# Hybrid encoder, first mixer: projecting each attention group in two parts, with three attention blocks between them

## Chip, cores and metric

The kernel runs on one core of one Trainium2 chip. The metric is the device time of one execution in microseconds (us). Engines: PE (TensorE), DVE (VectorE), ACT (ScalarE), POOL (GpSimd), and SP, whose queue issues most of the DMAs.

## What is computed

Two encoder layers over 1024 tokens of width 1024. Each has a token mixer and a gated feed-forward network. The change touches the first mixer alone: windowed attention with 16 query heads of 64 in four groups that share one key/value head each, rotary position, one sink per head, and beside it four cross-attention heads of 128 into 256 memory tokens.

```
q, k, v, xq = split(u @ w_in, [1024, 1280, 1536])
q, k = rope(q), rope(k)                    # v: no rotary
# block n of 128 queries sees keys of blocks n-1, n, n+1, |i - j| <= 128
s = q @ k.T * d ** -0.5 ;  m = max(max(s), sink)
p = exp(s - m) / (sum(exp(s - m)) + exp(sink - m))
o = p @ v
y = concat([o, memory_cross_attn(xq, mem_kv)]) @ w_out
```

## The kernel before

Every product of fp32 precision is built from high and low parts: `split` (lines 85 to 87) copies a tile to its high part on ACT and subtracts it on DVE for the low part, and `mm3` (lines 80 to 83) issues three matmuls. The normalised input stands transposed in `uh` and `ul`.

The tokens are eight tiles of 128. For each group of heads `proj(g)` (line 252) loads four weight units (`wunit`, line 69, in a ring of four slots), and for each tile `t` multiplies 24 times into a PSUM bank `pj` of 384 columns (lines 81 to 83, two such banks), applies the rotary products on DVE (lines 274 and 275), adds them on POOL into `rq` (lines 276 and 277), and splits the values (lines 279 and 280). After four tiles it turns them: PE transposes `rq` into the one bank `ptq` (line 286), first the two pairs of query heads and then the keys, and ACT and DVE split them into `qs` (lines 294 to 297) and into `kh`, `kl`. Keys and values of even and odd groups lie in different pools, so two groups can be alive at once.

`attend(g)` (line 300) goes through eight blocks `n` of 128 queries. A block takes, for each of four heads, two score matmuls into one of two `ps` banks (lines 315 and 316) and a masked maximum on DVE (line 318); then exponentials on ACT (line 325), scaling on ACT and DVE (lines 331 and 333), transposes into `pt` (line 338), `split` into `ph`, `pl`, two value products into the one bank `po` (lines 341 and 342) and an output sum (lines 344 and 345). Inner blocks have 384 keys, the first and last 256. Two blocks at a time go to `oT` in DRAM.

A cross unit (`cross_unit`, line 185) is one cross head and half of the tokens: 24 matmuls of 512 columns into a `pj` bank, a split into `xh`, `xl` (one buffer), scores into `ps`, a maximum (line 204), exponentials, transposes and products with the memory's values. There are eight; `XU` says how many stand behind each half of a group's attention.

The program's text is projection and attention in turn, group after group. A scheduler turns it into one fixed order for each engine: it takes what is ready, earlier text first, so that products of the next group fill attention's waits. The release of the pools that hold `pj` and `ptq` after the last projection gives their banks to the output projection `WOut` (line 371), whose `open` runs products into banks `pb` beside the last attention. Weights for the output projection take the same ring.

Of the kernel before, what the change touches and what calls it, by code (L numbers as in the profile page):

```python
# [6 lines left out]
F32 = mybir.dt.float32  # L7
# [9 lines left out]
P = 128  # L17
T = 1024
# [12 lines left out]
MEM_POOL = 1  # L31
QKV_POOL = (0, 2, 2, 2)

XU = [(0, 2), (0, 2), (2, 2), (0, 0)]
HX = [(0,) * 6, (0,) * 6] + [(0, 0, 1, 1, 0, 0), (0,) * 6] * 2 + [(0, 0, 1, 1, 0, 0), (0, 1, 1, 0, 0, 0)]


# [9 lines left out]
def build(tc, A, out):  # L47
# [37 lines left out]
    def split(h, l, src):  # L85
        act.copy(h, src)  # L86
        dve.tensor_tensor(l, src, h.bitcast(F32), op=ALU.subtract)  # L87
# [139 lines left out]
    def window():  # L227
# [21 lines left out]

        units = [(h, b) for h in range(4) for b in range(2)]  # L250

        def proj(g):
            us = [wunit(A["wqkv"][g, u], 768, eng=pool if u < QKV_POOL[g] else None) for u in range(4)]
            qs = [[None] * 2 for _ in range(4)]
            kvp = ap_ if g % 2 else ea
            kh = kvp.tile([P, T], F32R, tag="kh", bufs=1, name="kh")
            kl = kvp.tile([P, T], F32R, tag="kl", bufs=1, name="kl")
            v = kvp.tile([P, NT, P], F32R, tag="v", bufs=1, name="v")
            for b in range(2):
                rqs = []  # L260
                for tt in range(4):
                    t = 4 * b + tt
                    ps = psq.tile([P, 384], F32, tag="pj", bufs=2, name="pj")
                    for k in range(KT):
                        wh, wl = us[k // 2]
                        c = slice((k % 2) * 384, (k % 2 + 1) * 384)
                        m = slice(t * P, (t + 1) * P)
                        mm3(ps, uh[:, k, m], ul[:, k, m], wh[:, c], wl[:, c], k == 0, k == KT - 1)
                    t1 = ea.tile([P, 320], F32, tag="t1", bufs=1, name="t1")
                    t2 = ea.tile([P, 320], F32, tag="t2", bufs=1, name="t2")  # L270
                    rq = ea.tile([P, 384], F32, tag="rq", bufs=5, name="rq")
                    cb = bc(cos[:, t, :].unsqueeze(1).unsqueeze(1), [P, 5, 2, 32])
                    sb = bc(sin[:, t, :, :].unsqueeze(1), [P, 5, 2, 32])
                    dve.tensor_tensor(c4(t1), c4(ps[:, :320]), cb, op=ALU.mult)
                    dve.tensor_tensor(c4(t2), c4(ps[:, :320])[:, :, ::-1, :], sb, op=ALU.mult)
                    pool.tensor_tensor(rq[:, :320], t1, t2, op=ALU.add)
                    done = pool.tensor_tensor(rq[:, 320:], t1[:, 256:], t2[:, 256:], op=ALU.add)
                    sum_steps[0].send(done)
                    act.copy(v[:, t, :64], ps[:, 320:])
                    dve.tensor_tensor(v[:, t, 64:], ps[:, 320:], v[:, t, :64].bitcast(F32), op=ALU.subtract)  # L280
                    rqs.append(rq)
                hs = slice(b * 512, (b + 1) * 512)
                for w in range(3):
                    tp = psq.tile([P, 4, P], F32, tag="ptq", bufs=1, name="ptq")
                    for tt in range(4):
                        pe.transpose(tp[:, tt, :], rqs[tt][:, w * P:(w + 1) * P], ident)
                    tp = tp.rearrange("p a b -> p (a b)")
                    if w == 2:
                        split(kh[:, hs], kl[:, hs], tp)
                    else:  # L290
                        lo, hi = slice(0, 64), slice(64, 128)
                        q0, q1 = [ap_.tile([P, 512], F32R, tag="qs", bufs=8, name="qs") for _ in range(2)]
                        qs[2 * w][b], qs[2 * w + 1][b] = q0, q1
                        act.copy(q0[lo], tp[lo])
                        dve.tensor_tensor(q0[hi], tp[lo], q0[lo].bitcast(F32), op=ALU.subtract)
                        act.copy(q1[hi], tp[hi])
                        dve.tensor_tensor(q1[lo], tp[hi], q1[hi].bitcast(F32), op=ALU.subtract)
            return qs, kh, kl, v

        def attend(g, qkv):  # L300
            qs, kh, kl, v = qkv
            for b in range(2):
                for nn in range(4):
                    if nn % 2 == 0:
                        o = ap_.tile([64, 4, 256], F32, tag="o", bufs=2, name="o")
                    n = 4 * b + nn
                    lo, hi = max(n - 1, 0), min(n + 2, NT)
                    w = (hi - lo) * P
                    mo = (lo - (n - 1)) * P
                    sm = ap_.tile([P, 4, 384], F32, tag="sm", bufs=3, name="sm")  # L310
                    st = {x: ap_.tile([P, 4], F32, tag=x, name=x) for x in ("mx", "nm", "es", "su", "rd")}
                    for j in range(4):
                        s = psp.tile([P, 384], F32, tag="ps", bufs=2, name="ps")
                        m = slice(nn * P, (nn + 1) * P)
                        pe.matmul(s[:, :w], qs[j][b][:, m], kh[:, lo * P:hi * P], start=True, stop=False)
                        pe.matmul(s[:, :w], qs[j][b][:, m], kl[:, lo * P:hi * P], start=False, stop=True)
                        hd = 4 * g + j
                        dve.tensor_tensor_reduce(out=sm[:, j, :w], in0=s[:, :w], in1=wmask[:, mo:mo + w],
                                                 scale=1.0, scalar=sk8[:, hd:hd + 1], op0=ALU.add, op1=ALU.max,
                                                 accum_out=st["mx"][:, j:j + 1])  # L320
                    dve.tensor_scalar_mul(st["nm"], st["mx"], -0.125)
                    dve.tensor_tensor(st["es"], sk[:, 4 * g:4 * g + 4], st["nm"], op=ALU.add)
                    act.activation(st["es"], st["es"], AF.Exp)
                    for j in range(4):
                        act.activation(sm[:, j, :w], sm[:, j, :w], AF.Exp, bias=st["nm"][:, j:j + 1], scale=0.125,
                                       accum_out=st["su"][:, j:j + 1])
                    dve.tensor_tensor(st["su"], st["su"], st["es"], op=ALU.add)
                    dve.reciprocal(st["rd"], st["su"])
                    for j in range(4):
                        if j < 2:  # L330
                            act.activation(sm[:, j, :w], sm[:, j, :w], AF.Copy, scale=st["rd"][:, j:j + 1])
                        else:
                            dve.tensor_scalar_mul(sm[:, j, :w], sm[:, j, :w], st["rd"][:, j:j + 1])
                    po = psp.tile([P, 4, P], F32, tag="po", bufs=1, name="po")
                    for c in range(hi - lo):
                        tp = psp.tile([P, 4, P], F32, tag="pt", bufs=2, name="pt")
                        for j in range(4):
                            pe.transpose(tp[:, j, :], sm[:, j, c * P:(c + 1) * P], ident)
                        ph, pl = pair("p", c)
                        split(ph, pl, tp.rearrange("p a b -> p (a b)"))  # L340
                        pe.matmul(po, v[:, lo + c, :], ph, start=c == 0, stop=False)
                        pe.matmul(po, v[:, lo + c, :], pl, start=False, stop=c == hi - lo - 1)
                    ov = o[:, :, (nn % 2) * P:(nn % 2 + 1) * P]
                    act.copy(ov, po[64:])
                    dve.tensor_tensor(ov, po[:64], ov, op=ALU.add)
                    if nn % 2 == 1:
                        ts_ = slice((n - 1) * P, (n + 1) * P)
                        for hp in range(2):
                            nc.sync.dma_start(
                                oT[0][2 * g:2 * g + 2, hp * 64:(hp + 1) * 64, ts_].rearrange("a d t -> d a t"),  # L350
                                o[:, hp::2, :])
                for _ in range(XU[g][b]):
                    xh_, xb_ = units.pop(0)
                    if xb_ == 0:
                        xhead[0] = cross_head(0, xh_, ea, ea.tile([P, 2, 256], F32, tag="kv", bufs=1, name="kv"))
                    cross_unit(0, xh_, xb_, xhead[0], ap_, tags, ea, pair)

        cur = proj(0)
        dve.tensor_scalar_mul(sk8, sk, 8.0)
        for g in range(3):  # L360
            attend(g, cur)
            cur = proj(g + 1)
        psq.release()
        ea.release()
        attend(3, cur)
        wo0.open(3, 2)
        psp.release()
        ap_.release()
# [1004 lines left out]
```

## Time and profile before

| | |
|---|---|
| median of 3 runs | 2715.87 us (2713.88 to 2719.8) |
| profiled execution | 2715.91 us |
| its span | 2714.1 us |
| mean granted PE clock | 0.992 |
| busy: PE, DVE, ACT, POOL | 97%, 67%, 51%, 17% |
| first mixer, about | 67 to 497 us of the span |

Lines of the profile name the line of the kernel, the engine, the operation, the output and inputs by the program's names, and shapes. Matmuls overlap: PE counts as busy while any matmul is in flight, so that a busy PE need not be issuing at its densest rate. The granted clock is 1.00 at full speed. Idle time in front of an instruction stands in square brackets with what ended it.

### The profile page before, as it was taken

To read this page: it belongs to the slowest core of one execution; us is meant where nothing else is said; L and a number is where in the kernel's file an instruction comes from. 1 tells how busy PE (TensorE), PEld (TensorE's weight loads), DVE (VectorE), ACT (ScalarE), POOL (GpSimd) and SP (SyncE) were. 2 spreads that over 40 slices of the span, in tenths; PEclk is the share of its full clock that TensorE was granted. 3 is DMA by queue.
4 is the path that set the end of the run, shared out by engine and by line. 5 is a ranking of instruction groups with operands and counts; after the bars stand their busy time and mean duration, and the time that the engine had idled before them with its cause. 6 is when DMAs were issued, how large, how long until landed. Compare 5 with 4: busy or idle time off the path is not lost. (4 is left out here: it accounts for less than half of the span.)

```text
span 2714.1 us, 39502 instructions
## 1 busy us (share of the span) xinstructions
PE 2638.7 (97%) x14496; PEld 2204.5 (81%) x14496; DVE 1828.5 (67%) x3042; ACT 1391.6 (51%) x2556; POOL 468.4 (17%) x520
## 2 busy tenths in 40 slices
PE   8999999999999999999999999999899999999998
PEld 7888887788888888887877888878688788888887
DVE  6588787678565565487695768769567756566447
ACT  6367667545444444454454545545454544444443
POOL 1231110211111100031132222212121111110013
PEclk9999999999999999999999999999999999999999
DMA  7683213667777757673243432111476777775666
GB/s 284 209 179 84 60 52 100 188 190 181 210 197 196 205 149 255 195 256 124 69 150 106 111 88 67 52 51 34 125 219 174 188 209 206 202 201 155 226 194 233
DMA packets 215316, 432.25 MB, mean 159 GB/s; under 512 B 20561, under 2 KB 77265, under 8 KB 209489
## 3 DMA queue, kind: packets, MB, share of 16 engines
q1 hardware_dynamic: 188128, 335.07, 38.3%
q0 software_dynamic: 24544, 90.19, 15.9%
q10 hardware_dynamic: 2448, 4.46, 0.4%
q8 instruction: 114, 1.87, 0.3%
q14 instruction: 82, 0.66, 0.1%
HBM read 335.79 MB, written 117.96 MB: 167 GB/s over the span
## 5 line engine op out<-in xcount | busy, mean ns | idle before, releaser
L87 DVE TENSOR_TENSOR wl<-st,wh 128x1024 fp32r<-128x1024 f32 (+1 forms) x238 | 262.6, 1110 | 326.7 <-ACT wh L86 321.6
L86 ACT CAST wh<-st 128x1024 fp32r<-128x1024 f32 (+1 forms) x238 | 222.5, 937 | 295.9 <-PE X L535 195.9
L81 PE MATMUL pj<-uh,wh 128*128 128x512 f32 x512 | 205.2, 401 | 6.3 <-DVE xl L87 2.5
L535 PE MATMUL X<-wl,wh 128*128 128x512 f32 x528 | 204.8, 390 | 0.3 <-DVE wl L87 0.3
L535 PE MATMUL X<-wh,wl 128*128 128x512 f32 x528 | 204.6, 389 | 0.0
L82 PE MATMUL pj<-ul,wh 128*128 128x512 f32 x512 | 202.7, 396 | 0.1
L83 PE MATMUL pj<-uh,wl 128*128 128x512 f32 x512 | 202.2, 395 | 0.0
L535 PE MATMUL X<-wh 128*128 128x512 f32 x528 | 198.8, 390 | 1.4 <-ACT c L908 1.1
L81 PE MATMUL pj<-wh,uh 128*128 128x384 f32 (+1 forms) x512 | 190.4, 373 | 0.4 <-DVE v L280 0.4
L82 PE MATMUL pj<-wl,uh 128*128 128x384 f32 (+1 forms) x512 | 186.4, 364 | 0.0
L83 PE MATMUL pj<-wh,ul 128*128 128x384 f32 (+1 forms) x512 | 186.3, 365 | 0.0
L77 DVE TENSOR_TENSOR wl<-st,wh 128x1024 fp32r<-128x1024 f32 (+1 forms) x92 | 119.0, 1301 | 23.3 <-ACT wh L76 22.8
L535 PE MATMUL V<-uh,wh 128*128 128x512 f32 x344 | 133.8, 389 | 0.0
L535 PE MATMUL V<-ul,wh 128*128 128x512 f32 x344 | 133.8, 389 | 0.0
L535 PE MATMUL V<-uh,wl 128*128 128x512 f32 x344 | 133.8, 389 | 0.0
L76 ACT CAST wh<-st 128x1024 fp32r<-128x1024 f32 (+1 forms) x99 | 100.1, 1016 | 50.8 <-PE pj L82 31.0
L81 PEld LDWEIGHTS pj<-uh,wh 128*128 128x128 f32 x512 | 97.4, 190 | 26.7 <-DVE xl L87 2.9
L535 PEld LDWEIGHTS X<-wh 128*128 128x128 f32 x528 | 99.1, 188 | 22.8 <-ACT c L908 1.5
L535 PEld LDWEIGHTS X<-wl,wh 128*128 128x128 f32 x528 | 99.1, 188 | 21.0 <-DVE wl L87 0.7
L535 PEld LDWEIGHTS X<-wh,wl 128*128 128x128 f32 x528 | 99.1, 188 | 20.7
L1134 POOL TENSOR_TENSOR E<-EP,q 128x256 f32<-128x256 f32 x64 | 49.2, 769 | 372.3 <-DVE EP L1127 280.3
L83 PEld LDWEIGHTS pj<-uh,wl 128*128 128x128 f32 x512 | 97.0, 189 | 19.6
(347 smaller groups left out, 7274.4 us busy)
## 6 DMA issues: line engine op xcount, KB each, us to landing
st<-hid SPq DMA_DIRECT2D x154, 256.0 KB, 3.1
st<-in_ffw_dram SPq DMA_DIRECT2D x108, 256.0 KB, 3.1
w2s<-in_ffw_dram POOLq DMA_DIRECT2D x24, 1024.0 KB, 7.9
st<-in_ffw_dram SPq DMA_DIRECT2D x46, 512.0 KB, 4.1
hid<-tt SPq DMA_DIRECT2D x88, 256.0 KB, 4.6
st<-w2s SPq DMA_DIRECT2D x88, 256.0 KB, 3.3
sx<-in_ffw_dram SPq DMA_DIRECT2D x84, 256.0 KB, 3.9
sy<-in_ffw_dram SPq DMA_DIRECT2D x42, 512.0 KB, 6.3
```

The source lines that it names most:

```text
L76: act.copy(h[:, :n], raw)
L77: (eng or dve).tensor_tensor(l[:, :n], raw, h[:, :n].bitcast(F32), op=ALU.subtract)
L81: pe.matmul(o, ah, bh, start=first, stop=False)
L82: pe.matmul(o, ah, bl, start=False, stop=False)
L83: pe.matmul(o, al, bh, start=False, stop=last)
L86: act.copy(h, src)
L87: dve.tensor_tensor(l, src, h.bitcast(F32), op=ALU.subtract)
L535: pe.matmul(o, x, y, start=new, stop=e, skip_group_check=not first)
L1134: pool.tensor_tensor(gl, pl_, ql, op=ALU.mult)
```

## The change

The function `proj` becomes a class with two methods: `project(t)` computes one tile, and `turn(b)` transposes and splits one half, now keys first and then the two pairs of query heads. `attend` takes a list of blocks. The order of the text in each group is: five tiles, the turn of the first half, attention blocks 0 to 2, three tiles, the turn of the second half, and for groups 0 to 2 attention blocks 3 to 7 and cross units. The cross units stand behind the whole of a group's attention, 2, 2 and 4 of them; before it was 2 behind the second half of groups 0 and 1, and 2 behind each half of group 2. In group 3, blocks 3 to 7 follow the release of the two pools, as all eight blocks did before. The arithmetic of a tile, a block and a unit is unchanged. The core of the diff:

```diff
-XU = [(0, 2), (0, 2), (2, 2), (0, 0)]
+XU = (2, 2, 4)
...
-                for w in range(3):
+                for w in (2, 0, 1):
...
-                for _ in range(XU[g][b]):
+        def cross(n):
+            for _ in range(n):
...
-        cur = proj(0)
-        dve.tensor_scalar_mul(sk8, sk, 8.0)
-        for g in range(3):
-            attend(g, cur)
-            cur = proj(g + 1)
+        cur = Group(0)
+        for g in range(4):
+            for t in range(5):
+                cur.project(t)
+            if g == 0:
+                dve.tensor_scalar_mul(sk8, sk, 8.0)
+            cur.turn(0)
+            attend(cur, range(0, 3))
+            for t in range(5, 8):
+                cur.project(t)
+            cur.turn(1)
+            if g < 3:
+                attend(cur, range(3, 8))
+                cross(XU[g])
+                cur = Group(g + 1)
         psq.release()
         ea.release()
-        attend(3, cur)
+        attend(cur, range(3, 8))
         wo0.open(3, 2)
```

More of the change, by code (lines that the diff above doesn't have):

```diff
@@ L250, in window @@
         units = [(h, b) for h in range(4) for b in range(2)]
[L252 to L281, printed above, removed]
@@ new lines, in window, with __init__, project, turn @@
+        class Group:
+            def __init__(self, g):
+                self.g = g
+                self.us = [wunit(A["wqkv"][g, u], 768, eng=pool if u < QKV_POOL[g] else None) for u in range(4)]
+                self.qs = [[None] * 2 for _ in range(4)]
+                kvp = ap_ if g % 2 else ea
+                self.kh = kvp.tile([P, T], F32R, tag="kh", bufs=1, name="kh")
+                self.kl = kvp.tile([P, T], F32R, tag="kl", bufs=1, name="kl")
+                self.v = kvp.tile([P, NT, P], F32R, tag="v", bufs=1, name="v")
+                self.rqs = {}
+            def project(self, t):
+                v = self.v
+                ps = psq.tile([P, 384], F32, tag="pj", bufs=2, name="pj")
+                for k in range(KT):
+                    wh, wl = self.us[k // 2]
+                    c = slice((k % 2) * 384, (k % 2 + 1) * 384)
+                    m = slice(t * P, (t + 1) * P)
+                    mm3(ps, uh[:, k, m], ul[:, k, m], wh[:, c], wl[:, c], k == 0, k == KT - 1)
+                t1 = ea.tile([P, 320], F32, tag="t1", bufs=1, name="t1")
+                t2 = ea.tile([P, 320], F32, tag="t2", bufs=1, name="t2")
+                rq = ea.tile([P, 384], F32, tag="rq", bufs=5, name="rq")
+                cb = bc(cos[:, t, :].unsqueeze(1).unsqueeze(1), [P, 5, 2, 32])
+                sb = bc(sin[:, t, :, :].unsqueeze(1), [P, 5, 2, 32])
+                dve.tensor_tensor(c4(t1), c4(ps[:, :320]), cb, op=ALU.mult)
+                dve.tensor_tensor(c4(t2), c4(ps[:, :320])[:, :, ::-1, :], sb, op=ALU.mult)
+                pool.tensor_tensor(rq[:, :320], t1, t2, op=ALU.add)
+                done = pool.tensor_tensor(rq[:, 320:], t1[:, 256:], t2[:, 256:], op=ALU.add)
+                sum_steps[0].send(done)
+                act.copy(v[:, t, :64], ps[:, 320:])
+                dve.tensor_tensor(v[:, t, 64:], ps[:, 320:], v[:, t, :64].bitcast(F32), op=ALU.subtract)
+                self.rqs[t] = rq
+            def turn(self, b):
@@ L282, in proj @@
                 hs = slice(b * 512, (b + 1) * 512)
-                for w in range(3):
+                for w in (2, 0, 1):
                     tp = psq.tile([P, 4, P], F32, tag="ptq", bufs=1, name="ptq")
                     for tt in range(4):
-                        pe.transpose(tp[:, tt, :], rqs[tt][:, w * P:(w + 1) * P], ident)
+                        pe.transpose(tp[:, tt, :], self.rqs[4 * b + tt][:, w * P:(w + 1) * P], ident)
                     tp = tp.rearrange("p a b -> p (a b)")
@@ L288, in proj @@
                     if w == 2:
-                        split(kh[:, hs], kl[:, hs], tp)
+                        split(self.kh[:, hs], self.kl[:, hs], tp)
                     else:
@@ L292, in proj @@
                         q0, q1 = [ap_.tile([P, 512], F32R, tag="qs", bufs=8, name="qs") for _ in range(2)]
-                        qs[2 * w][b], qs[2 * w + 1][b] = q0, q1
+                        self.qs[2 * w][b], self.qs[2 * w + 1][b] = q0, q1
                         act.copy(q0[lo], tp[lo])
@@ L297, in proj @@
                         dve.tensor_tensor(q1[lo], tp[hi], q1[hi].bitcast(F32), op=ALU.subtract)
[L298 to L311, printed above, removed]
-                    for j in range(4):
[L313 to L351, printed above, removed]
-                for _ in range(XU[g][b]):
[L353 to L356, printed above, removed]
@@ L358, in window, with attend @@
-        cur = proj(0)
-        dve.tensor_scalar_mul(sk8, sk, 8.0)
-        for g in range(3):
-            attend(g, cur)
-            cur = proj(g + 1)
+        def attend(x, blocks):
+            g, qs, kh, kl, v = x.g, x.qs, x.kh, x.kl, x.v
+            for n in blocks:
+                b, nn = divmod(n, 4)
+                if nn % 2 == 0:
+                    x.o = ap_.tile([64, 4, 256], F32, tag="o", bufs=2, name="o")
+                o = x.o
+                lo, hi = max(n - 1, 0), min(n + 2, NT)
+                w = (hi - lo) * P
+                mo = (lo - (n - 1)) * P
+                sm = ap_.tile([P, 4, 384], F32, tag="sm", bufs=3, name="sm")
+                st = {x: ap_.tile([P, 4], F32, tag=x, name=x) for x in ("mx", "nm", "es", "su", "rd")}
+                for j in range(4):
+                    s = psp.tile([P, 384], F32, tag="ps", bufs=2, name="ps")
+                    m = slice(nn * P, (nn + 1) * P)
+                    pe.matmul(s[:, :w], qs[j][b][:, m], kh[:, lo * P:hi * P], start=True, stop=False)
+                    pe.matmul(s[:, :w], qs[j][b][:, m], kl[:, lo * P:hi * P], start=False, stop=True)
+                    hd = 4 * g + j
+                    dve.tensor_tensor_reduce(out=sm[:, j, :w], in0=s[:, :w], in1=wmask[:, mo:mo + w],
+                                             scale=1.0, scalar=sk8[:, hd:hd + 1], op0=ALU.add, op1=ALU.max,
+                                             accum_out=st["mx"][:, j:j + 1])
+                dve.tensor_scalar_mul(st["nm"], st["mx"], -0.125)
+                dve.tensor_tensor(st["es"], sk[:, 4 * g:4 * g + 4], st["nm"], op=ALU.add)
+                act.activation(st["es"], st["es"], AF.Exp)
+                for j in range(4):
+                    act.activation(sm[:, j, :w], sm[:, j, :w], AF.Exp, bias=st["nm"][:, j:j + 1], scale=0.125,
+                                   accum_out=st["su"][:, j:j + 1])
+                dve.tensor_tensor(st["su"], st["su"], st["es"], op=ALU.add)
+                dve.reciprocal(st["rd"], st["su"])
+                for j in range(4):
+                    if j < 2:
+                        act.activation(sm[:, j, :w], sm[:, j, :w], AF.Copy, scale=st["rd"][:, j:j + 1])
+                    else:
+                        dve.tensor_scalar_mul(sm[:, j, :w], sm[:, j, :w], st["rd"][:, j:j + 1])
+                po = psp.tile([P, 4, P], F32, tag="po", bufs=1, name="po")
+                for c in range(hi - lo):
+                    tp = psp.tile([P, 4, P], F32, tag="pt", bufs=2, name="pt")
+                    for j in range(4):
+                        pe.transpose(tp[:, j, :], sm[:, j, c * P:(c + 1) * P], ident)
+                    ph, pl = pair("p", c)
+                    split(ph, pl, tp.rearrange("p a b -> p (a b)"))
+                    pe.matmul(po, v[:, lo + c, :], ph, start=c == 0, stop=False)
+                    pe.matmul(po, v[:, lo + c, :], pl, start=False, stop=c == hi - lo - 1)
+                ov = o[:, :, (nn % 2) * P:(nn % 2 + 1) * P]
+                act.copy(ov, po[64:])
+                dve.tensor_tensor(ov, po[:64], ov, op=ALU.add)
+                if nn % 2 == 1:
+                    ts_ = slice((n - 1) * P, (n + 1) * P)
+                    for hp in range(2):
+                        nc.sync.dma_start(
+                            oT[0][2 * g:2 * g + 2, hp * 64:(hp + 1) * 64, ts_].rearrange("a d t -> d a t"),
+                            o[:, hp::2, :])
@@ new lines, in cross @@
+        def cross(n):
+            for _ in range(n):
+                xh_, xb_ = units.pop(0)
+                if xb_ == 0:
+                    xhead[0] = cross_head(0, xh_, ea, ea.tile([P, 2, 256], F32, tag="kv", bufs=1, name="kv"))
+                cross_unit(0, xh_, xb_, xhead[0], ap_, tags, ea, pair)
+        cur = Group(0)
[13 more added lines that the diff above has]
+                cur = Group(g + 1)
```

## The prediction

> **What bounds the kernel now.** I read the page first, then the busy time by stretches of the first mixer, then TensorE's (PE's) timeline inside them, then VectorE's (DVE's) groups. From the page, the span and PE's line:
>
> ```profile
> span 2714.1 us, 39502 instructions
> PE 2638.7 (97%) x14496; PEld 2204.5 (81%) x14496; DVE 1828.5 (67%) x3042; ACT 1391.6 (51%) x2556; POOL 468.4 (17%) x520
> ```
>
> PE is the bound, but "busy" is a union of overlapping matmuls, so I price PE by the distance between starts in dense stretches. From PE's timeline (start, duration, instruction):
>
> ```profile
> 313.01 0.39 PE L82 MATMUL pj<-ul,wh 128*128 128x512 f32 x1
> 313.24 0.39 PE L83 MATMUL pj<-uh,wl 128*128 128x512 f32 x1
> 322.46 0.28 PE L83 MATMUL ps<-kvh,xl 128*128 128x256 f32 x1
> 322.58 0.28 PE L81 MATMUL ps<-kvh,xh 128*128 128x256 f32 x1
> 395.37 0.60 PE L217 MATMUL pt<-ident,xp 128*128 128x128 f32 x4
> 395.80 0.60 PE L286 MATMUL ptq<-ident,rq 128*128 128x128 f32 x4
> 398.00 0.33 PE L82 MATMUL pj<-wl,uh 128*128 128x384 f32 x1
> 398.17 0.33 PE L83 MATMUL pj<-wh,ul 128*128 128x384 f32 x1
> ```
>
> A matmul costs 0.23 us at 512 columns, 0.17 at 384, 0.12 at 256, and a transpose 0.11 (0.43 for four). I call the sum of instructions at these prices dense work. Next the stretches of the mixer (start:end, length, busy time of each engine, granted clock, DMA):
>
> ```profile
> 70.00:80.00 10.00, 7.44 (x42) 6.96 (x41) 3.59 (x8) 0.98 (x3) 2.83 (x4) 1.00 0.50 146
> 100.00:115.00 15.00, 10.99 (x50) 9.49 (x49) 11.11 (x26) 7.39 (x18) 9.54 (x12) 0.77 0.52 169
> 115.00:313.47 198.47, 194.23 (x1112) 172.50 (x1111) 154.51 (x426) 135.10 (x349) 38.95 (x52) 1.00 0.53 132
> 313.47:326.05 12.58, 9.92 (x55) 7.29 (x53) 11.63 (x40) 10.79 (x32) 0.00 (x0) 1.00 0.01 2
> 326.05:402.18 76.13, 75.36 (x448) 69.67 (x449) 58.01 (x155) 50.75 (x133) 9.93 (x14) 0.98 0.12 32
> 402.18:428.68 26.50, 18.65 (x73) 12.45 (x71) 22.67 (x64) 20.79 (x51) 1.14 (x2) 0.81 0.42 136
> 428.68:480.00 51.32, 51.32 (x258) 43.35 (x259) 34.38 (x93) 32.52 (x81) 0.00 (x0) 1.00 0.34 97
> ```
>
> Counting PE's records in these rows at the dense prices gives 6.8, 7.7, 184.8, 8.2, 71.9, 11.1 and 50.0 us. The losses are therefore 3.2, 7.3, 13.7, 4.3, 4.2, 15.4 and 1.3 us. Two rows show one state: at 313 and at 402 PE has only attention to do, and DVE is busy 92% and 86% of the time. Everywhere else PE is nearly full and DVE waits. So the mixer's time is its dense work plus what is lost where attention has no projection or output product to run beside it. A change of order can win or lose only there.
>
> DVE's instructions in the mixer, by form (line, operation, output and input, count, busy us, mean ns of one, idle before); these means are the prices below:
>
> ```profile
> L87 DVE TENSOR_TENSOR pl<-pt,ph 128x512 fp32r<-128x512 f32 x104 | 70.6, 683 | 22.4 <-ACT ph L86 22.1
> L318 DVE CUSTOM_DVE_ANT_0 sm<-ps,wmask,sk 128x384 f32<-128x384 f32 x96 | 57.2, 610 | 16.4 <-PE ps L316 14.2 <-PE pt L338 1.7
> L345 DVE TENSOR_TENSOR o<-po,o 64x512 f32<-64x512 f32 x32 | 21.7, 679 | 7.9 <-ACT o L344 7.8
> L333 DVE TENSOR_SCALAR sm<-sm,rd 128x384 f32<-128x384 f32 x48 | 18.5, 427 | 0.4
> L318 DVE CUSTOM_DVE_ANT_0 sm<-ps,wmask,sk 128x256 f32<-128x256 f32 x32 | 14.5, 475 | 2.1 <-PE ps L316 2.1
> L297 DVE TENSOR_TENSOR qs<-ptq,qs 64x512 fp32r<-64x512 f32 x16 | 11.1, 693 | 4.7 <-ACT qs L296 4.4
> L204 DVE TENSOR_REDUCE nm<-ps 128x2 f32<-128x512 f32 x16 | 10.7, 682 | 0.5 <-PE ps L83 0.4
> L318 DVE DVE_READ_ACCUMULATOR2_ANT mx<- 128x1 f32 x128 | 10.3, 80 | 0.0
> L322 DVE TENSOR_TENSOR es<-sk,nm 128x4 f32<-128x4 f32 x32 | 5.6, 174 | 0.3
> L274 DVE TENSOR_TENSOR t<-pj,cos 128x320 f32<-128x320 f32 x32 | 15.5, 484 | 12.9 <-PE pj L83 12.7
> L87 DVE TENSOR_TENSOR ol<-or,oh 128x768 fp32r<-128x768 f32 x6 | 5.7, 958 | 4.1 <-ACT oh L86 4.1
> L77 DVE TENSOR_TENSOR xwl<-st,xwh 128x1024 fp32r<-128x1024 f32 x2 | 2.4, 1216 | 0.0
> L87 DVE TENSOR_TENSOR ol<-or,oh 128x256 fp32r<-128x256 f32 x5 | 2.1, 426 | 0.9 <-ACT oh L86 0.8
> ```
>
> **What the change moves.** Arithmetic, instruction counts and DMAs stay. The scheduler writes out an order for each engine. Between the two programs these orders differ, outside the mixer, in the first products of the following FFN only, by exchanges inside a stretch where PE is full, which I price at nothing. The cross heads' loads on SP's queue move with their units, but their weights are still split ahead of group 2's first scores, and the DMA share in the row from 313 is 0.01, so I price that at nothing too. Four places in the mixer remain.
>
> *First projection.* Before, the first transpose of `rq` stands right behind the second tile's products and waits for GpSimd. In the new order a whole third tile (24 matmuls, 4.1 us) stands between.
>
> ```profile
> 77.79 0.33 PE L286 MATMUL ptq<-ident,rq 128*128 128x128 f32 x1 [2.11 <-POOL rq L276]
> 78.56 0.41 PE L81 MATMUL pj<-wh,uh 128*128 128x384 f32 x1 [0.45 <-DVE v L280]
> ```
>
> Both waits go: -2.6 us; 4.1 us of cover against 2.1 needed, and nothing else is late.
>
> *First attention blocks.* Before, the blocks wait for the last key split; these are two of the waits that make the row from 100:
>
> ```profile
> 106.19 0.50 PE L315 MATMUL ps<-kh,qs 128*128 128x256 f32 x2 [1.14 <-ACT kh L86]
> 109.02 0.45 PE L286 MATMUL ptq<-ident,rq 128*128 128x128 f32 x1 [2.33 <-DVE kl L87]
> ```
>
> In the new order keys are turned first and the first score product stands inside the last tile, so these two waits go. But the fifth score product needs one of two `ps` banks back, and DVE's queue has a query split, a weight split and two rotary products ahead of the reduction that frees it: 0.69 + 1.2 + 1.0 + 0.6, about 3.5 us. Bounds: 0 to -7.3 (the whole loss of the row); I take -2.3, the loss less this wait and 1.5 us of slow clock (the value is nearer to the waits of the row that stay in kind than to nothing lost).
>
> *Group 2.* This is the largest term. A cross unit's query product stays in a `pj` bank until the `x` operands of the unit before are used, and there are two such banks. With three units' products issued, two wait in both banks, and no projection tile of group 3, nor the fourth unit, can start until the second unit's operands are split. That split waits for the first unit's scores. Before, units 5 and 6 (of 8) stand behind block 3 of group 2, so only 12.58 us pass:
>
> ```profile
> 326.05 0.50 PE L81 MATMUL pj<-uh,wh 128*128 128x512 f32 x1 [2.49 <-DVE xl L87]
> 314.63 0.61 DVE L318 CUSTOM_DVE_ANT_0 sm<-ps,wmask,sk 128x384 f32<-128x384 f32 x1
> 325.31 0.69 DVE L87 TENSOR_TENSOR xl<-pj,xh 128x512 fp32r<-128x512 f32 x1 [0.24 <-ACT xh L86]
> ```
>
> With all four units behind block 7, the scores of the first of them stand behind blocks 3 to 7. The new PE order between the last product of the third unit and the first of the fourth has 34 score products at 384 and 8 at 256, 63 transposes, 33 value products, 4 turns and 12 cross scores: 5.8 + 1.0 + 6.9 + 7.5 + 0.4 + 1.4 = 23.1 us dense. DVE's share, by the groups above: 17 wide and 4 narrow reductions with their reads 10.4 + 1.9 + 1.7; 14 splits 9.6; 11 scalings 4.6; 5 output sums 3.4; two query splits, one `x` split and two cross maxima 3.4; 26 small ones 4.4: 39.4 us. What that takes is read from the same stretch of before, where the same count gives 13.4 us from the reduction at 314.63 on: the split ends at 326.00, 11.4 us later (0.85 of the sum, since instructions overlap), and 12.6 us pass from PE's last product (0.94). For 39.4 that is 33.5 and 37.0; I take 35.3. The loss is 35.3 - 23.1 = 12.2 against 4.3 now: +7.9. Ends: 33.5 gives +6.1, the full 39.4 gives +12.0. Nothing gives it back: after it PE has projection and cross work for 60 us, but before that work ran with 4.2 us lost in 76, so there was little to save.
>
> *The end.* In group 3 the halves come too late to help. The scheduler puts the first score products of block 0 into the last two tiles only, so seven blocks still follow the last projection, with the output projection's products (`pb`) as the only cover. Before, these begin in earnest at 428.68. In the new order they begin behind the scores of block 5, where DVE has 38.6 us of instructions since the last tile, against 28.3 before. That is: 19 reductions with reads (12.9), 7 splits (4.8), 10 scalings (4.1), 2 output sums, 4 query and 1 key splits (4.7), 3 weight splits (3.6), 5 operand splits of the output projection (two at 768 columns, two at 512, one at 256: 3.7), 20 small (3.4), one tile's rotary (1.4). Before, 28.3 took 26.5 (0.94): now 36.2. Dense PE work in it is 17.1 (11.1 before), so the loss is 19.1 against 15.4: +3.7. At 0.85 it is 32.8 and +0.3; at the full sum +6.1.
>
> Sum: -2.6 - 2.3 + 7.9 + 3.7 = +6.7. The profiled execution took 2715.91 us (span 2714.1 and 1.8 around it), equal to the median of 2715.87; so 2722.6, say **2723**. By the faster pace alone it would be -2.6 - 2.3 + 6.1 + 0.3 = +1.5.
>
> [...] In the row from 313 the granted clock is 1.00 with PE busy 79%; in the rows from 100 and 402 it is 0.77 and 0.81, though the longest single wait in the first is 2.33 us. [...]
>
> **Rivals.**
> *The clock falls through group 2's stretch.* If PE ran it at half speed, its 23.1 us would be 46.2, more than DVE's 35.3: 2722.6 + 10.9 = 2733.5. For it: 0.81 in the row from 402, where PE is busy 70%. Against: 1.00 in the same stretch of before.
>
> *Faster.* Every half now keeps three tiles in reserve while attention runs. If that ended the scattered losses (13.7 us in 115 to 313 and 4.2 in 326 to 402), the time would be 2722.6 - 17.9 = 2704.7. It decides once 12.2 of these 17.9 us go. Against: DVE has the same work there (154.51 of 198.47 us), and before, eight tiles of the next group are in reserve already.
>
> *No change.* At the faster pace, and with the opening's waits gone wholly (-7.3 for -2.3): -2.6 - 7.3 + 6.1 + 0.3 = -3.5, or 2712.4; with the -2.3 it is 2717.4.
>
> *The change does not do what it says.* Partly so, and counted above: in groups 1 and 2 the scheduler mixed next tiles into attention before, and in group 3 the blocks come too late.
>
> **How the numbers follow.** About 0.2% (5.4 us) is what a measurement of this kernel can tell from no change: 2710.5 to 2721.3. Forecast 0.55, clock 0.08, no change 0.24, faster 0.13. The forecast's own ends are -2.6 - 7.3 + 6.1 + 0.3 = -3.5 and -2.6 + 0 + 12.0 + 6.1 = +15.5, so 2712 to 2731; its middle lies above 2721.3, and a small part of it is moved to "same" against the clock's share. The range takes in the clock's 2733.5 and stops short of the faster case: 2711 to 2735. Slower 0.62, same 0.25, faster 0.13.
>
> **What would show it.** Right: the waits at 77.79 and 109.02 are gone; in group 2 one stretch of 33 to 40 us without a `pj` matmul in which DVE is over 85% busy, ended by a wait of PE for `xl`; the next 60 us nearly dense; behind the last tile more than 26.5 us to dense `pb` work. Wrong: that stretch under 25 us, the clock under 0.9 in it, or PE's loss from 115 to group 2's block 2 far from 13.7.

## The result, and the profile after

The changed kernel takes 2731.27 us (median of 5 runs, 2727.25 to 2733.16) against 2715.87 (5 runs, 2711.23 to 2719.8) before: a ratio of 1.0055, 95% interval 1.0041 to 1.0069. It is slower, by 15.4 us where 6.7 were forecast. The kernel before also ran beside every experiment below; over those later runs its median lies at 2718.1 to 2718.9. The changed kernel did not run beside those; against them the difference would be 13 us.

The first lines of the page after:

```profile
span 2729.5 us, 39511 instructions
PE 2645.6 (97%) x14496; PEld 2210.9 (81%) x14496; DVE 1827.6 (67%) x3042; ACT 1392.7 (51%) x2556; POOL 466.0 (17%) x520
```

The work is the same: equal counts of matmuls and of DVE instructions, DVE as busy as before. What grew is time in which PE issues nothing. The stretches of the mixer after, cut at the same events as in the prediction (start:end, length, busy time of each engine, granted clock, DMA):

```profile
100.00:115.00 15.00, 11.56 (x58) 10.44 (x57) 9.90 (x24) 7.66 (x17) 9.30 (x12) 0.83 0.45 138
115.00:315.24 200.24, 194.52 (x1118) 174.32 (x1117) 158.09 (x437) 137.11 (x356) 38.77 (x52) 1.00 0.53 132
315.24:353.88 38.64, 31.10 (x157) 22.00 (x155) 32.40 (x104) 33.01 (x90) 0.00 (x0) 0.96 0.08 21
353.88:415.68 61.80, 59.51 (x354) 55.66 (x354) 36.82 (x86) 28.43 (x71) 9.02 (x14) 1.00 0.11 35
415.68:444.50 28.82, 19.44 (x76) 14.51 (x76) 26.78 (x72) 22.80 (x60) 2.12 (x2) 0.76 0.46 149
444.50:510.00 65.50, 62.71 (x313) 51.92 (x313) 39.65 (x98) 41.14 (x95) 0.00 (x0) 1.00 0.30 80
```

The third row is the one to read: 38.6 us in which PE has only attention, where the same place took 12.58 us before. PE's timeline at its two ends, and DVE's at the second:

```profile
315.01 0.39 PE L83 MATMUL pj<-uh,wl 128*128 128x512 f32 x1
...
353.88 0.50 PE L81 MATMUL pj<-uh,wh 128*128 128x512 f32 x1
...
353.14 0.68 DVE L87 TENSOR_TENSOR xl<-pj,xh 128x512 fp32r<-128x512 f32 x1
```

No `pj` product starts between 315.01 and 353.88, and the one at 353.88 starts 0.06 us after the split of the unit before it ends (353.14 + 0.68). The fourth row shows why the time is not given back. PE is full there, but DVE is busy 36.82 of 61.80 us, 60%, where in the corresponding stretch before (the row from 326.05) it was busy 58.01 of 76.13. Attention had been worked off in the third row, so the projections that were held back now ran with little attention beside them.

What PE lost by stage, in us: length less its matmuls at the dense prices, counted anew in all four kernels in the same way (for before this gives 12.9 for the stretch that the prediction put at 13.7). The two kernels on the right are the first two experiments below.

| stage | before | changed | halves only | units only |
|---|---|---|---|---|
| 60 to 115 | 9.9 | 9.6 | 9.0 | 10.7 |
| 115 to group 2's stretch | 12.9 | 13.8 | 14.1 | 14.4 |
| that stretch | 4.2 | 15.0 | 3.1 | 16.6 |
| from there to the last tile | 4.2 | 3.6 | 3.7 | 8.9 |
| last tile to dense `pb` work | 15.5 | 17.3 | 19.4 | 17.9 |
| to the end of the mixer's losses | 5.9 | 4.2 | 2.2 | 5.0 |
| sum | 52.6 | 63.5 | 51.5 | 73.5 |

The first product of the next stage (`X`, in the feed-forward network) moves from 594.36 to 606.01 us, by 11.65. The other 3.7 us of the profiled difference lie behind it: 2.8 of them at one place in the network, where a wait of PE is 1.2 us longer (2.23 for 1.06) and a lower clock follows (1.00 at the same place before):

```profile
1062.00:1079.00 17.00, 14.77 (x59) 11.84 (x58) 7.41 (x12) 8.48 (x16) 0.00 (x0) 0.90 0.57 191
```

### The profile page after: what moved, and what is told of

Its sections match the earlier page's. It is cut to its first block, busy times and chain, and to the rows that moved or that the text cites. A ratio compares the mean times of both kernels' runs of the same rounds, so it can differ in the third digit from the quotient of the medians.

```text
span 2729.5 us, 39511 instructions
## 1 busy us (share of the span) xinstructions
PE 2645.6 (97%) x14496; PEld 2210.9 (81%) x14496; DVE 1827.6 (67%) x3042; ACT 1392.7 (51%) x2556; POOL 466.0 (17%) x520
```

## The experiments

Theory 1: the four cross units behind block 7 of group 2 cost the time, because units whose products are issued hold both `pj` banks until the one buffer of `x` operands is free. Theory 2: the halves cost it. Theory 3: the loss lies outside the mixer. After the first four runs theory 1 was split: 1a, a freed bank gives its gain to the time; 1b, what PE gains by running ahead of attention is owed where the projections end.

### The two parts of the change, each alone

Halves only:

```diff
-XU = (2, 2, 4)
+XU = ((0, 2), (0, 2), (2, 2))
...
-                attend(cur, range(3, 8))
-                cross(XU[g])
+                attend(cur, range(3, 4))
+                cross(XU[g][0])
+                attend(cur, range(4, 8))
+                cross(XU[g][1])
```

> The changed kernel with the cross units of group 2 put back to two behind block 3 and two behind block 7; the halves stay in all four groups. Theory 1 (the four units behind block 7 are the cost: PE lost 15.5 us in the 38.6 us without a projection product, against about 5 in the kernel before): that stretch shrinks to 12 to 15 us and the time falls by about 10, to 2721 (2718 to 2724). Theory 2 (the halves cost it: keys turned first, three tiles held back): it stays at 2728 or above. Theory 3 (the loss is outside the mixer, a clock drop in the first FFN): it stays within 3 us of the changed kernel's 2731.

Units only, on the kernel before:

```diff
-XU = [(0, 2), (0, 2), (2, 2), (0, 0)]
+XU = [(0, 2), (0, 2), (0, 4), (0, 0)]
```

> The kernel before, whole groups, with only the cross units of group 2 all behind block 7. Theory 1: in the new order 48 score products, 28 value products, 54 transposes and 12 cross scores stand between the third and the fourth unit, 21.6 us dense; a stretch of 34 to 38 us without a projection product, 12 to 16 us lost there against 4.3, time 2725 to 2728. Theory 2 (halves): 2714 to 2718, no change. Theory 3: no change in the mixer, 2716.

Measured: halves only 2717.21 us, just under theory 1's range, ratio to before 0.9995 (0.9986 to 1.0004); units only 2736.49, ratio 1.0071 (1.0059 to 1.0084). Group 2's stretch in halves only, then in units only:

```profile
315.77:326.75 10.98, 9.05 (x53) 6.66 (x51) 9.37 (x28) 9.46 (x25) 0.00 (x0) 1.00 0.08 24
```

```profile
315.83:354.88 39.05, 30.39 (x149) 22.06 (x147) 32.95 (x111) 32.66 (x91) 0.00 (x0) 0.91 0.07 14
354.88:423.10 68.22, 64.58 (x360) 59.09 (x361) 36.45 (x80) 29.54 (x74) 8.10 (x12) 0.95 0.10 32
```

The stretch comes and goes with the units' place, and the time with it. Theories 2 and 3 fall: the halves alone cost nothing. Whether they save something beside the four units is not shown, since the ratios of the changed kernel (1.0041 to 1.0069) and of units only overlap. Units only costs 18 us, 6 more than the upper end that was expected: its stretch takes 39 us where 34 to 38 were expected, and in the 68 us behind it 8.9 are lost where the changed kernel loses 3.6, again with DVE little busy (36.45 of 68.22).

### The same four units in group 1

```diff
-XU = (2, 2, 4)
+XU = (2, 4, 2)
```

> The changed kernel with the four units behind block 7 of group 1 and two behind that of group 2. Theory 1 (four units in a row hold both pj banks through blocks 3 to 7, wherever they stand): one stretch of 36 to 40 us without a projection product in group 1 and none over 15 us in group 2; about 10 us lost against halves_only, 2727 (2724 to 2731). Rival: only late in the mixer is it not given back, since here two more groups of projections follow in which attention can catch up: 2716 to 2720.

Measured: 2724.74 us, ratio 1.0019 (1.0010 to 1.0029).

```profile
225.68:262.12 36.44, 28.93 (x147) 21.68 (x146) 29.91 (x97) 31.62 (x88) 0.00 (x0) 0.91 0.07 15
262.12:315.00 52.88, 50.57 (x301) 46.89 (x300) 31.79 (x77) 23.76 (x65) 7.32 (x12) 1.00 0.33 73
```

The stretch is there, in group 1, with 14.5 us lost, and no stretch of over 8 us in group 2. The time lies in theory 1's range, at its lower end, and above the rival's. Counted as in the table, the mixer loses 59.5 us, 6.9 more than before, though the stretch alone lost 14.5: with more groups to come some of the loss is given back, not all.

### Taking away what holds the banks

Three buffers for the `x` operands. The room for them came from the load of the memory's keys and values, first by sharing the units' output buffer, then by a buffer of the weights' stage:

```diff
-            pl, n = (ea, 1) if kind == "x" else (ap_, 2)
+            pl, n = (ea, 3) if kind == "x" else (ap_, 2)
...
-... ea.tile([P, 2, 256], F32, tag="kv", bufs=1, name="kv"))
+... ea.tile([P, 512], F32, tag="xo", bufs=1, name="kv").rearrange("p (a b) -> p a b", a=2))        # x_three
+... stg.tile([P, 1024], F32, tag="st", name="kv")[:, :512].rearrange("p (a b) -> p a b", a=2))    # x_three_stage
```

> The changed kernel with three buffers in place of one for the x operands of the cross units (to make room, the memory's keys and values are loaded into the buffer of the units' output, so a head's load waits for the output of the unit before). This takes away what holds the pj banks. Theory 1: no stretch of over 15 us without a projection product in group 2; the last units' scores then fall behind the last tile, where PE has 24.8 us dense beside about 34 of DVE, a loss of 9 against 17.7 in the changed kernel: 2731 - 14 - 8 = 2709, at most 2719 if the tail gains nothing. If the units' place alone matters and not the bank: stays at 2726 or above.

> The changed kernel with three buffers for the x operands, as in x_three, but the memory's keys and values now go through a buffer of the weights' stage and not through the units' output. x_three had no stretch in group 2 but two new waits of 5.7 and 6.2 us behind a head's load. Theory 1a (what PE loses is set by the bank alone): those waits go too, 2717 to 2719 at most, less if the tail wins. Theory 1b (attention that PE runs ahead of is owed, and is paid where the projections end): the waits go (-12), but behind the last tile PE has 23 us dense beside about 48 us of DVE, 45 at 0.94, so 22 us are lost there as against 17.7 in the changed kernel: 2721 (2718 to 2726).

Measured: the first 2733.73 us, ratio 1.0060 (1.0047 to 1.0072); the second 2713.61, ratio 0.9985 (0.9975 to 0.9995). Neither has such a stretch in group 2: no gap between projection products there is longer than 8 us. The first still missed theory 1's time and lies where the units' place alone was to put it. The second, with the units in the same place, rules that reading out; what the first has in addition is a load that waits for the output of the unit before. PE's and ACT's timelines there:

```profile
415.05 0.80 PE L81 MATMUL ps<-kvh,xh 128*128 128x256 f32 x2 [6.19 <-ACT kvh L86]
...
408.90 0.58 ACT L223 COPY xo<-po 128x512 f32<-128x512 f32 x1 [1.67 <-PE po L83]
...
414.38 0.62 ACT L86 CAST kvh<-kv 128x512 fp32r<-128x512 f32 x1 [4.90 <-DMA kv<-kvd]
```

The output is copied at 408.9, stored, and only then the next head's load may start; ACT and PE stand for 5 to 6 us. With the load through the stage these waits are gone, and so is the whole loss of the change. The stretches of the second kernel:

```profile
115.00:260.00 145.00, 144.81 (x856) 135.04 (x855) 114.20 (x308) 93.94 (x246) 35.17 (x47) 1.00 0.62 153
315.00:381.10 66.10, 65.33 (x394) 59.36 (x393) 57.72 (x167) 53.66 (x143) 7.03 (x12) 1.00 0.15 36
381.10:425.00 43.90, 34.52 (x158) 24.83 (x156) 38.61 (x107) 32.50 (x86) 2.19 (x2) 0.88 0.40 124
425.00:505.00 80.00, 76.25 (x366) 62.18 (x365) 47.05 (x110) 49.71 (x115) 4.78 (x4) 0.98 0.39 110
```

PE is busy in all of 115 to 260, and the last tile ends at 381 instead of 402 (before) or 416 (changed). But 43.9 us pass from there to dense `pb` work, against 26.5 before. Of the 17.4 us more, 4.8 are lost (20.3 for 15.5) and the rest is PE work that stood ahead of the last tile before. The loss there is near the 22 that 1b gave. The time is all the same below 1b's range, and what 1a gave as its upper end holds.

### What is owed at the end

Halves only with two `x` buffers, and the kernel before with its last two units moved behind group 3's last tile:

```diff
-XU = [(0, 2), (0, 2), (2, 2), (0, 0)]
+XU = [(0, 2), (0, 2), (2, 0), (0, 0)]
...
         for g in range(3):
             attend(g, cur)
             cur = proj(g + 1)
+        cross(2)
         psq.release()
```

> The halves with the units of group 2 in their old places (halves_only), and two x buffers, keys and values through the stage. In x_three the second buffer took the scattered losses of groups 0 and 1 from 11 us (130 to 260 us) to 2. Theory 1a: that gain is kept, 2717 - 9 = 2708. Theory 1b: attention then lags by as much, the last stretch grows by about 9, and the time stays at 2715 to 2719.

> The kernel before with the last two cross units moved from behind block 7 of group 2 to behind group 3's last tile, ahead of the release of its pools: two units only behind block 3, so one pj bank stays free in group 2, and cross scores stand beside the attention of group 3. If a stretch costs what DVE needs at 0.94 less PE's dense work: group 2's loss of 4.3 goes, and behind the last tile PE has 14.6 us dense against about 25 (10 lost for 15.4): 2706 (2702 to 2712). Rival: the output projection waits for the last unit, and what is won is lost behind it: 2714 or above.

Measured: 2718.11 us, ratio 0.9993 (0.9984 to 1.0001), and 2718.82 us, ratio 1.0000 (0.9991 to 1.0009). No gain in either. The first, 115 to 260 and group 2's stretch:

```profile
115.00:260.00 145.00, 143.71 (x849) 133.77 (x848) 114.10 (x305) 93.19 (x242) 33.57 (x46) 1.00 0.61 149
307.27:329.70 22.43, 18.42 (x89) 13.37 (x87) 20.67 (x70) 20.38 (x57) 0.00 (x0) 0.92 0.25 83
```

It loses 8 us less than halves only in 115 to 260; then group 2's stretch grows from 11.0 to 22.4 us, since with two buffers a third unit can be issued early and the fourth and the tiles still wait. Between 260 and 370 us it loses 9 more than halves only: what was won is paid there. The time is that of 1b, but not the place: behind 370 us the two kernels lose about the same, and it is the banks in group 2 that take the gain. The second, group 2 and the start of what follows:

```profile
310.00:370.00 60.00, 59.68 (x362) 55.68 (x361) 47.67 (x136) 40.53 (x114) 5.80 (x10) 1.00 0.12 35
370.00:390.00 20.00, 14.87 (x72) 12.37 (x72) 15.80 (x36) 13.76 (x31) 6.06 (x6) 0.83 0.36 106
```

Group 2's stretch is gone, as expected, and 8.2 us are lost at 370 to 390 in its stead. From 400 to 430 it loses another 13.9, where 10 were expected behind the last tile. So the rival's time came, though not for its reason: the output projection's first product starts at 427.0 (425.8 before), and the loss lies ahead of it.

The same three buffers with whole groups and the old units:

> The kernel before, whole groups and its own cross units, with three x buffers and the keys and values through the stage: what x_three_stage has beside the halves and the units' place. If with free banks the groups' order and the units' place no longer matter, as theory 1b has it (VectorE's work sets the sum of the losses): the scattered losses go, the last stretch grows by as much, 2713 to 2717, equal to x_three_stage within 3 us. If the halves do win once the bank is free: 2718 or above, x_three_stage 4 us faster.

Measured: 2720.97 us, ratio 1.0011 (1.0003 to 1.0020), outside the first expectation and inside the second: 0.26% above the changed kernel with three buffers. So three buffers win nothing where the units stand as before; what they win on the changed kernel is the loss that the change made. Whether the halves make the 0.26% stays open: the units' place differs too, and the variants with three buffers lose some 5 us at varying places. PE waits once for 4.30 us in this run, at a place where x_three_stage has no wait (first line below). In the profile of x_three_pool_w below, ACT stands at 193 for a weight (second line) whose load landed only then: the two loads of that kind issued between 170 and 196 landed 15.3 us after their issue (median), where one between 170 and 200 in the changed kernel took 5.9. In x_three_stage the same cast runs at 189.76 without such a wait; why the load was slow is not shown:

```profile
187.85 0.88 PE L286 MATMUL ptq<-ident,rq 128*128 128x128 f32 x3 [4.30 <-DVE kl L87]
...
192.96 0.83 ACT L76 CAST wh<-st 128x768 fp32r<-128x768 f32 x1 [5.47 <-DMA st<-in_wqkv_dram]
```

### Work taken off VectorE

One of its two scalings per block on GpSimd (on the kernel before), and the low parts of the output projection's weights on GpSimd (on the kernel before, on x_three_stage, and there with both):

```diff
-                            dve.tensor_scalar_mul(sm[:, j, :w], ...)
+                            (dve if j == 2 else pool).tensor_scalar_mul(sm[:, j, :w], ...)
...
-    wunit(A[self.key][b, u], pl=self.w1 if i >= RING else None)
+    wunit(A[self.key][b, u], pl=self.w1 if i >= RING else None, eng=pool if self.l == b == 0 else None)
```

> The kernel before with one of VectorE's two scalings of each block on GpSimd: 32 instructions less on VectorE, 13.7 us by their groups, and 32 more on GpSimd, which is busy 39 of 198 us in groups 0 to 2 and 1 of 26 behind the last tile. If VectorE's sum sets every stretch in which PE has only attention (0.94 of it): about a twentieth of VectorE's work goes, the stretch in group 2 and the one behind the last tile shorten by some 2 us, the scattered waits by as much: 2712 to 2714. If the chain of one block sets them and not VectorE's sum, GpSimd's slower scaling (its additions of 320 columns take 0.92 us where VectorE's scaling takes 0.43) makes it no faster: 2716 to 2720.

> The kernel before with the low parts of the output projection's first six weights on GpSimd, nothing else. Theory 1b: the stretch behind the last tile (26.5 us, VectorE 86% busy) holds some of these splits, 3 to 5 us less on VectorE: 2711 to 2715. If it changes nothing: 2716 to 2719.

> x_three_stage with the low parts of the output projection's first six weights made on GpSimd in place of VectorE: five of them, 6.1 us, lie in the last stretch (381 to 425 us), where VectorE is busy 88% and GpSimd 2 of 44 us. Theory 1b (VectorE's sum sets the last stretch): it shortens by 5, 2713.6 - 5 = 2708 to 2709. If the chain through TensorE and ScalarE sets it: 2713 as before.

> x_three_pool_w with one of VectorE's two scalings of each block on GpSimd as well, as in pool_scale (32 instructions, 13.7 us less on VectorE). Theory 1b: three more us in the last stretch and a few of the rest, 2704 to 2707. If GpSimd's slower scaling lies on the chain of a block: 2709 or above.

Measured: pool_scale 2716.42 us, ratio 0.9991 (0.9981 to 1.0001); before_pool_w 2720.40, 1.0010 (1.0001 to 1.0019); x_three_pool_w 2719.34, 1.0001 (0.9990 to 1.0011); x_three_pool_ws 2719.90, 1.0008 (0.9999 to 1.0017). None brought the gain that 1b expected; the first lies in its second expectation, the others at or above what was expected without a gain. In x_three_pool_w, DVE and POOL at the end of the last stretch:

```profile
424.02 4.78 DVE L337 TENSOR_SCALAR sm<-sm,rd 128x384 f32<-128x384 f32 x2
...
423.78 4.80 POOL L77 TENSOR_TENSOR xwl<-st,xwh 128x1024 fp32r<-128x1024 f32 x2 [30.32 <-ACT xwh L76]
...
429.39 0.69 PE L319 MATMUL ps<-kh,qs 128*128 128x384 f32 x1 [3.70 <-DVE mx L322]
```

Two scalings that take 0.4 us each elsewhere last as long as GpSimd's two splits beside them, 4.8 us, and PE waits 3.7 for the reduction behind them. In this run the work was not taken off VectorE's path but put in front of it in another way, and the last section shows the same in before_pool_w. So the runs with these splits say little on whether VectorE's sum sets the last stretch.

## Why the prediction was right, and where it was not

*Direction, and the largest term.* Right in mechanism and place. One stretch without `pj` work of 38.6 us (33 to 40 forecast) with DVE busy 84% of it (over 85% forecast), ended by the `xl` split, and nearly dense work behind it. The count of instructions was right too: 17 wide and 4 narrow reductions, 14 splits. Mis-sized was the pace: 39.4 us of DVE instructions took 38.6, a factor of 0.98 where 0.85 to 0.94 was read from before. So the loss is 15.0 where 12.2 was forecast, and the term +10.8 where +7.9 was (ends 6.1 and 12.0). Of the 3.3 us above the 35.3 that were forecast, a single wait of DVE makes 2.19; in the stretch of before, from 314.63 on, none of its waits is over 0.4 us:

```profile
339.58 0.75 DVE L337 TENSOR_SCALAR sm<-sm,rd 128x384 f32<-128x384 f32 x2
342.52 0.16 DVE L331 TENSOR_TENSOR su<-su,es 128x4 f32<-128x4 f32 x1 [2.19 <-ACT es L327]
...
342.30 0.19 ACT L327 ACTIVATE es<-es 128x4 f32<-128x4 f32 x1
...
343.73 0.66 PE L342 MATMUL pt<-ident,sm 128*128 128x128 f32 x4 [3.14 <-DVE pl L87]
```

ACT runs a small exponential behind four large ones and two scalings; DVE's queue stands behind it, and PE behind DVE. A pace read from a 12 us stretch did not contain such a turn.

*First projection, -2.6.* Failed. The step said that nothing else is late. The wait of 2.11 for `rq` went, and the third tile, put in front of it, now waits as long for a bank (first row) and starts where it did before, at 78.62 for 78.56. The next two rows are further down, in the first attention blocks:

```profile
78.62 0.41 PE L81 MATMUL pj<-wh,uh 128*128 128x384 f32 x1 [2.13 <-DVE v L283]
...
108.22 0.39 PE L319 MATMUL ps<-kh,qs 128*128 128x256 f32 x1 [0.95 <-DVE qs L300]
...
111.22 0.58 PE L319 MATMUL ps<-kh,qs 128*128 128x256 f32 x1 [2.49 <-DVE qs L302]
```

Behind the wait at 78.62 the clock was lower, which it was not before. The same 3.4 us after, then before:

```profile
78.60:82.00 3.40, 3.38 (x12) 3.40 (x13) 1.11 (x3) 0.21 (x1) 3.11 (x6) 0.59 0.58 210
```

```profile
78.60:82.00 3.40, 3.40 (x20) 3.40 (x21) 1.01 (x3) 0.21 (x1) 2.26 (x4) 1.00 0.79 277
```

Eight matmuls fewer at 0.17 us each are about 1.4 us.

*First attention blocks, -2.3.* Failed: the waits were replaced. The keys' waits at 106.19 and 109.02 went, and the query splits, now turned last, are waited for instead (second and third row above). The queue of DVE that the step names was there, and the two waits sum to 3.4 us, near its 3.5; but it held back the second query split, not a `ps` bank. Both terms together: 9.9 lost before, 9.6 after, where 4.9 were to be won. Behind 115 us slow matmuls go on (granted clock 0.50 and 0.62 in the first two us, 1.00 before) and lose some 0.9 us that the kernel before does not lose there, so that in all nothing was won.

*The end, +3.7.* Failed in size: 28.8 us from the last tile to dense `pb` work, where 36.2 were forecast; the loss there is 1.8 larger and behind it 1.7 smaller, +0.1 in all. The pace was right: the DVE instructions in the stretch sum to 30.6 us, and 28.8 is 0.94 of that. What was wrong is how far the list reaches, 38.6 us: six scalings and three operand splits of it run behind 444.5, when `pb` work is already dense, and PE's dense work ahead of it is 11.5 us, not 17.1.

*The sum.* -0.3 (opening), +0.9 (from 115 on, the slow matmuls behind the opening), +10.8, -0.6 (to the last tile), +0.1 (end): +10.9 of lost time; the mixer's end moved by 11.65. So the forecast's +6.7 held two gains that did not come and an end that did not worsen, and fell short in the main term. That the errors of the gains and of the end point in opposite directions is luck: it brings the sum nearer than its terms. What lies outside the mixer, some 3.7 us of the profiled difference, is within the scatter of single runs (2711.23 to 2719.8 before).

*The rivals.* The clock did not fall through the stretch: 0.96, where this rival was priced at half speed (0.50, the granted clock of the kernel before from 109 to 114). Scattered losses did not end (12.9 before, 13.8 after), though three `x` buffers show that they can (2.9 in 115 to 260, where 10.6 are lost before), and that little of it reaches the time.

*The clock.* In the stretch the matmuls behind the wait of 3.14 us start 0.43 us apart, where 0.23 is dense; the granted clock from 345 to 349 is 0.57:

```profile
345.63 0.63 PE L345 MATMUL po<-ph,v 128*128 128x512 f32 x1
346.06 0.63 PE L346 MATMUL po<-pl,v 128*128 128x512 f32 x1
346.49 1.05 PE L342 MATMUL pt<-ident,sm 128*128 128x128 f32 x4
```

Slow matmuls also follow the wait of 2.13 us in the opening (the granted clock of 0.59 above) and, in the kernel before, the waits of 2.33 us at 109.02 (0.50 from 109 to 114) and 2.49 us at 326.05 (0.57 from 326 to 330). Behind its 2.11 us at 77.79 the clock is 1.00. What sets the clock behind a wait, these runs do not show. The price of the slow matmuls in the stretch is, as an estimate from its mean clock of 0.96 over 38.6 us, about 1.5 us.

## What to carry to other kernels

Before moving work in the order, ask which buffer each piece holds while it waits, and what else needs that buffer: four units that were ready early held two banks, and with them 38 us of the projections. A wait that is taken away is worth only the distance to the next one on the same path: in the opening each removed wait was followed by one of the same length, and what PE won in the middle with more `x` buffers was mostly paid later, in group 2's stretch or where the projections ended. The cheap repair was two more small buffers, not another order; by their ratios to the kernel before, the changed kernel with them is 0.7% faster than without, and its 0.15% under the kernel before is less than the 0.2% that the prediction took as measurable.

## What was not expected of the hardware

VectorE's scaling of 384 columns from SBUF to SBUF takes 0.42 us in x_three_stage; the two that met GpSimd's splits of 1024 columns in x_three_pool_w took 2.43 us in the mean, as long as the splits (2.42). In before_pool_w an operand split of 768 columns took 2.64 us beside them, where it takes 0.95 in x_three_stage, while the split of `pt`, which lies in PSUM, took its usual 0.69:

```profile
428.15 4.71 POOL L77 TENSOR_TENSOR xwl<-st,xwh 128x1024 fp32r<-128x1024 f32 x2 [16.08 <-ACT xwh L76]
...
429.54 0.69 DVE L87 TENSOR_TENSOR pl<-pt,ph 128x512 fp32r<-128x512 f32 x1 [1.69 <-ACT ph L86]
...
431.03 2.64 DVE L87 TENSOR_TENSOR ol<-or,oh 128x768 fp32r<-128x768 f32 x1
```

What makes them long, no run here shows. The same split costs GpSimd twice what it costs VectorE (2.42 us in x_three_pool_w against 1.22 in x_three_stage).
